# Attention scores: the product with the keys' low part moved to 64-row halves of the matmul array

## The chip, the cores and the metric

The kernel runs on one core of one Trainium2 chip. The metric is the device time of one execution in microseconds; three runs of the kernel before give a median of 1186.78 us. TensorE (PE in the profile) multiplies, VectorE (DVE), ScalarE (ACT) and GpSimd (POOL) work element by element, and SyncE (SP) issues most of the DMA transfers. A matmul record is preceded by a record of its weight load (PEld).

## The reference, cut to what matters

One transformer block on 1024 tokens of width 1024: a normalized and modulated input goes through one projection into a recurrent branch and an attention branch, both are mixed back, and a mixture of 16 experts follows. The part that the change touches is the attention:

```python
q = rms_norm(q, g_q) * (HEAD_DK ** -0.5)
k = rms_norm(k, g_k)
...
s = jnp.einsum('bqhjd,bkhjd->bhjqk', qi, k).astype(jnp.float32) + bias[None, :, None]
p = jax.nn.softmax(s, axis=-1)
w = (p[:, :, 0] - lam * p[:, :, 1]).astype(v.dtype)
return jnp.einsum('bhqk,bkhd->bqhd', w, v)
```

There are 4 heads (h), each with two score maps (j = 0, 1) over 64 channels (d), and queries are taken in 8 blocks of 128. All data is float32.

## The kernel before, in words

Products in float32 are made from parts: a value is split into a high part of type float32r and a low part, the rest. Each of the two goes through TensorE in one pass, and the products of parts are summed in PSUM.

For the attention, `proj_qk` writes the normalized and transposed queries and keys of each head to DRAM as `qkd[kind, h][part, channel, token]`; kind 0 is the queries, kind 1 the keys; part 0 is the high part, part 1 the low one; channels 0 to 63 belong to j = 0 and 64 to 127 to j = 1. `prep_begin(h)` (L725) loads them back into SBUF by 64-row transfers from SyncE's queue (L732): `qs[j]` has the high part of the queries on rows 0 to 63 and their low part on rows 64 to 127; `kh[j]` has the keys' high part on both row halves, `kl[j]` their low part on both. Four transfers of 256 KB each make a pair of tiles. With `qs` stationary, a matmul against `kh` over 128 rows is high times high plus low times high, and one against `kl` is high times low plus low times low.

`sc_mm(g, j)` (L755) makes the scores of one query block and one j: g counts the 32 turns (head times query block). It issues four matmuls of 512 columns into a [128, 1024] PSUM tile: `kh` for both column halves, then `kl` for both. `sc_max` (L764) adds the bias and takes the minimum (the queries carry a minus sign) in one VectorE instruction of 1024 columns; `sc_exp` is the exponential on ScalarE.

The loop over g (L908) has its orders of TensorE, VectorE and ScalarE written out by hand; a planner orders SyncE and GpSimd. In turn g TensorE makes: 8 transposes of turn g-2's weights (`w_tr`, tile `pw`), `sc_mm(g+1, 0)`, 16 matmul records of turn g-3's product with the values (`pv_mm`, tile `pv`), `sc_mm(g+1, 1)`, and in every fourth turn 4 transposes of a finished output (`o_out`, tile `po`). VectorE makes two `sc_max`, a few instructions of one column, and one combination of the two maps over 1024 columns (L807); every fourth turn it also begins a reciprocal root (`o_rstd`, L845 on) that waits for squares made on GpSimd (L837). GpSimd also prepares the output projection's weights in that loop (`load_wo(k)`, L875: a transfer, 4 products with `gate1`, and after ScalarE's rounding 4 subtractions into `wol`). `gate1` (L904) lies in memory that comes free when the last matmul of the V projection (tile `pjv`) has ended.

Turn 0's scores (`sc_first`, L776) stand inside that last V projection: TensorE waits there for the loads of `prep_begin(0)`, whose order is `kh`, `kl`, bias, `qs`. For h = 1 to 3 `prep_begin` runs 8 turns ahead, in the order `qs`, `kh`, `kl`, bias.

Elsewhere `mod_out` (L626) issues matmuls whose stationary operand has 32 columns, at four different column positions of the array (tile `mq`); all matmuls of the attention use the whole array, and no matmul of this kernel uses fewer than 128 rows.

Of the kernel before, what the change touches and what calls it, by code (L numbers as in the profile page):

```python
# [8 lines left out]
F32 = mybir.dt.float32  # L9
# [9 lines left out]
P = 128  # L19
# [63 lines left out]
def tile_block(ctx: ExitStack, tc, x, cols, w_mod, b_mod, w_in, wa, wx, lam_qk, relT, w_out, g2, w_router,  # L83
               w1, w3, w2, jbits, jfrac, out):
    nc = tc.nc
    V, A, G_, T, SY = nc.vector, nc.scalar, nc.gpsimd, nc.tensor, nc.sync
# [5 lines left out]
    def mm(out, lhsT, rhs, start, stop):  # L92
        return T.matmul(out, lhsT=lhsT, rhs=rhs, start=start, stop=stop)  # L93
# [26 lines left out]
    qkd = {(kind, h): dram.tile([2, P, S], F32, name=f"qkd{kind}{h}") for kind in range(2) for h in range(NH)}  # L120
# [350 lines left out]
    with tc.issue_after(i_act.ins), tc.issue_after(i_pool.ins):  # L471
        A.dma_start(out=jb, in_=jbits)
        A.dma_start(out=jf, in_=jfrac)
        for gi, src in enumerate((wa, wx)):
            braw = lt_(f"bd{gi}", [P, 8, P])
            G_.memset(braw, 0.0)
            for par in range(2):
                A.dma_start(out=braw[par * 64:par * 64 + 64, :, par * 64:par * 64 + 64],
                            in_=src.rearrange("(n par) c d -> par c n d", par=2)[par])
# [223 lines left out]
    prs = {}  # L703
# [6 lines left out]
    def qk_one(tag, name, dt=F32, shape=None):  # L710
        return qkp.tile(shape or [P, S], dt, tag=f"qk{tag}", bufs=1, name=name)

    def qk_tile(name, dt=F32):
        tg = qk_slot[name]
        if tg == "c":
            t_ = qk_one(tg, name, dt, [P, 2, S])
            return t_[:, 0, :], t_[:, 1, :]
        return [qk_one(f"{tg}{j}", f"{name}_{j}", dt) for j in range(2)]
# [6 lines left out]
    def prep_begin(h):  # L725
        sets = {}

        def load(tg, kind, parts):
            t_ = sets[tg] = qk_tile(f"{tg}{h}", F32R) if h else qk0[f"{tg}0"]
            for j in range(2):  # L730
                for a in range(2):
                    SY.dma_start(out=t_[j].bitcast(F32)[64 * a:64 * a + 64, :], in_=qkd[kind, h][parts[a], 64 * j:64 * j + 64, :])  # L732

        def bias():
            bt = sets["b"] = ap.tile([P, 1920], F32, name=f"bias{h}", tag="bias", bufs=1) if h % 2 else \
                qk_one("c", f"bias{h}", F32, [P, 1920]) if h else qk0["bias0"]
            src = bvd[h, 0:1920]
            SY.dma_start(out=bt, in_=bass.AP(tensor=src.tensor, offset=src.offset, ap=[[1, P], [1, 1920]]))

        qs, kh, kl = ("qs", 0, (0, 1)), ("kh", 1, (0, 0)), ("kl", 1, (1, 1))  # L740
        if h:
            for q in (qs, kh, kl):
                load(*q)
            bias()
        else:
            load(*kh)
            load(*kl)
            bias()
            load(*qs)
        prs[h] = (sets["b"], [sets[tg] for tg in ("qs", "kh", "kl")])  # L750
# [3 lines left out]

    def sc_mm(g, j):  # L755
        h, qt = divmod(g, NT)
        qs, kh, kl = (t_[j] for t_ in prs[h][1])
        sc_ = psa.tile([P, S], F32, tag="sc", bufs=2, name=f"sc{g}_{j}") if g else psb.tile([P, S], F32, tag="pg", bufs=2, name=f"sc0_{j}")
        for i, kk in enumerate((kh, kl)):
            for n in range(2):  # L760
                mm(sc_[:, n * 512:(n + 1) * 512], qs[:, qt * P:(qt + 1) * P], kk[:, n * 512:(n + 1) * 512], i == 0, i == 1)
        scp[g, j] = sc_

    def sc_max(g, j):  # L764
# [11 lines left out]
    def sc_first():  # L776
        for j in range(2):
            sc_mm(0, j)
        for j in range(2):
            sc_max(0, j)  # L780
            sc_exp(0, j)

    prep_begin(0)
    with tc.manual_schedule(engines={mybir.EngineType.PE}):
        proj_v(wv1, 1, vt[2:4], sc_first, AA)
# [121 lines left out]
    with tc.manual_schedule(engines={mybir.EngineType.PE, mybir.EngineType.DVE, mybir.EngineType.Activation}):  # L907
        for g in range(NG + 2):  # L908
            hn, u = divmod(g, 8)
            if u == 0 and hn + 1 < NH:  # L910
                prep_begin(hn + 1)
# [7 lines left out]
            n, st = divmod(g - 8, 4)  # L919
            if st == 0 and 0 <= n < 6:  # L920
                o_rstd(n)
            if g < NG:
                if g:
                    sc_exp(g, 0)
                if g + 1 < NG:
                    sc_mm(g + 1, 0)
                if g:
                    sc_max(g, 1)
# [10 lines left out]
            if g < NG - 1:  # L939
                sc_mm(g + 1, 1)  # L940
            if g in (4, 8, 12, 16, 24, 26, 28, 30):
                load_wo({4: 0, 8: 1, 12: 2, 16: 3, 24: 4, 26: 5, 28: 6, 30: 7}[g])
            n, st = divmod(g - 6, 4)
            if st == 0 and 0 <= n < 7:
                o_evac(n)
            n, st = divmod(g - 10, 4)
# [316 lines left out]
    raws, used, parts, raw_l = {}, [0], {}, []  # L1263
# [198 lines left out]
```

## Time and profile before

| | us |
|---|---|
| three runs: median (lowest to highest) | 1186.78 (1185.78 to 1189.39) |
| the profiled execution, and its span | 1189.59, 1187.8 |
| TensorE busy over the span | 1115.3 (94%) |
| VectorE busy | 955.2 (80%) |
| ScalarE busy | 791.6 (67%) |
| GpSimd busy | 484.1 (41%) |
| mean granted TensorE clock | 0.979 of full |

The page gives the share of each engine. The stretches matter more than the shares: the projections and the recurrent branch fill the time up to about 322 us, the attention loop that up to about 474 us, the mixing and the routing that up to about 618 us, and the experts the rest. The chain of waits is the work that ended last, followed back from the end: what stands in it at a time is what set the pace there.

### The profile page before, as it was taken

The page shows a single profiled execution, that of the slowest core. Times are in us where ns is not written, and L with a number is a line of the kernel's source. Part 1 is how long each engine was busy: PE and PEld are TensorE (multiplying, and loading weights), DVE is VectorE, ACT ScalarE, POOL GpSimd, SP SyncE. Part 2 cuts the span into 40 slices and gives each one's busy share as a digit, 9 for nine tenths or more (in the row PEclk, how much of TensorE's full clock was granted, in tenths as well). Part 3 has the DMA queues.
Part 4 walks back from the last instruction along what each step waited for, and adds up shares of the span by engine and source line. Part 5 has one row for each costly group of instructions (what it writes and reads, how often), then busy time and mean ns, then how long its engine had stood idle before and what let it go on. Part 6 is the DMA issues. An engine that isn't in the chain of part 4 may idle for free.

```text
span 1187.8 us, 17864 instructions
## 1 busy us (share of the span) xinstructions
PE 1115.3 (94%) x6319; PEld 935.9 (79%) x6320; DVE 955.2 (80%) x1241; ACT 791.6 (67%) x1046; POOL 484.1 (41%) x540
## 2 busy tenths in 40 slices
PE   6999899999699999999649999999999999999996
PEld 4699898888588899777538788888888888888885
DVE  6797657874298897444579999999999999999995
ACT  7548282394177788544318788878887888888784
POOL 4693232133087547243544334443324444322400
PEclk9899999999899999999969999999999999999999
DMA  9765725723844604534799999999999999999911
GB/s 334 225 195 171 238 72 186 241 71 63 203 108 117 176 6 143 186 113 163 263 337 345 358 377 385 392 408 393 375 394 393 367 397 406 394 394 387 392 46 18
DMA packets 147889, 303.82 MB, mean 256 GB/s; under 512 B 17996, under 2 KB 44748, under 8 KB 147796
## 3 DMA queue, kind: packets, MB, share of 16 engines
q1 hardware_dynamic: 134864, 279.46, 65.9%
q0 software_dynamic: 5488, 19.45, 6.4%
q10 hardware_dynamic: 7448, 3.77, 1.1%
q8 instruction: 50, 0.82, 0.3%
q14 instruction: 39, 0.32, 0.1%
HBM read 277.42 MB, written 25.22 MB: 255 GB/s over the span
## 4 chain that ended last, share of the span: by engine, by line
PE 73%; DVE 7%; DMA 6%; POOL 6%; issue 5%; ACT 2%; SPq 0%; POOLq 0%; ACTq 0%; DVEq 0%
PE ab L93 28%; PE y L93 13%; PE mix L93 7%; PE pjk L93 3%; PE pjz L93 3%; PE pv L93 3%; PE sc L93 3%; POOL wo L886 2%; PE pjv L93 2%; DMA wr<-in_w_mod_dram 2%; PE pw L814 1%; PE pjx L93 1%; PE pf L1346 1%; PE pg L93 1%; DVE macc L624 1%
## 5 line engine op out<-in xcount | busy, mean ns | idle before, releaser
L1246 POOL TENSOR_SCALAR oh<-iot,slot 128x128 bf16<-128x128 bf16 x120 | 146.3, 1234 | 252.2 <-PE pf L1346 252.2
L93 PE MATMUL ab<-wh,xeh 128*128 128x512 f32 x512 | 202.0, 395 | 0.2 <-ACT xeh L90 0.2
L93 PE MATMUL ab<-wh,xel 128*128 128x512 f32 x512 | 199.7, 390 | 0.1
L93 PE MATMUL ab<-wl,xeh 128*128 128x512 f32 x512 | 157.7, 389 | 0.0
L93 PEld LDWEIGHTS ab<-wl,xeh 128*128 128x128 f32 x512 | 96.1, 188 | 20.3
L93 PEld LDWEIGHTS ab<-wh,xel 128*128 128x128 f32 x512 | 96.2, 188 | 19.4 <-DVE xel L1259 0.5
L93 PEld LDWEIGHTS ab<-wh,xeh 128*128 128x128 f32 x512 | 96.1, 188 | 19.4 <-ACT xeh L90 0.5
L142 DVE TENSOR_TENSOR wl<-w_0r,wh 128x1024 fp32r<-128x1024 f32 x79 | 96.8, 1226 | 10.2 <-ACT wh L90 0.4
L90 ACT ACTIVATE wh<-w_0r 128x1024 fp32r<-128x1024 f32 x81 | 86.0, 1062 | 24.9 <-PE ab L93 14.9
L142 DVE TENSOR_TENSOR wl<-w_3r,wh 128x1024 fp32r<-128x1024 f32 x79 | 96.6, 1224 | 6.2
L90 ACT ACTIVATE wh<-w_1r 128x1024 fp32r<-128x1024 f32 x79 | 83.5, 1058 | 23.6 <-PE ab L93 18.9
L90 ACT ACTIVATE wh<-w_3r 128x1024 fp32r<-128x1024 f32 x79 | 83.9, 1062 | 21.9 <-PE ab L93 18.2
L142 DVE TENSOR_TENSOR wl<-w_2r,wh 128x1024 fp32r<-128x1024 f32 x80 | 96.3, 1220 | 2.4 <-ACT wh L90 0.5
L90 ACT ACTIVATE wh<-w_2r 128x1024 fp32r<-128x1024 f32 x80 | 84.7, 1060 | 18.9 <-PE ab L93 17.9
L142 DVE TENSOR_TENSOR wl<-w_1r,wh 128x1024 fp32r<-128x1024 f32 x78 | 92.6, 1220 | 3.8 <-ACT wh L90 2.1
L768 DVE CUSTOM_DVE_ANT_0 p<-sc,bias 128x1024 f32<-128x1024 f32 x64 | 77.7, 1214 | 18.0 <-PE sc L93 18.0
L93 PE MATMUL y<-wh,htl 128*128 128x512 f32 x256 | 82.9, 395 | 0.0
L93 PE MATMUL y<-wh,hth 128*128 128x512 f32 x256 | 80.9, 396 | 0.0
L93 PE MATMUL y<-wl,hth 128*128 128x512 f32 x256 | 79.6, 391 | 0.0
L90 ACT ACTIVATE p<-p,stat 128x1024 f32<-128x1024 f32 x62 | 70.8, 1151 | 4.8 <-DVE stat L768 4.8
L93 PEld LDWEIGHTS pv<-v,wt 128*128 128x128 f32 x512 | 61.7, 192 | 2.4
L93 PE MATMUL pv<-v,wt 128*128 128x128 f32 x512 | 62.1, 275 | 0.0
(458 smaller groups left out, 2858.5 us busy)
## 6 DMA issues: line engine op xcount, KB each, us to landing
w_0r<-in_w_dram SPq DMA_DIRECT2D x81, 512.0 KB, 8.5
w_1r<-in_w_dram SPq DMA_DIRECT2D x79, 512.0 KB, 8.8
w_2r<-in_w_dram SPq DMA_DIRECT2D x78, 512.0 KB, 9.0
w_3r<-in_w_dram SPq DMA_DIRECT2D x77, 512.0 KB, 8.7
wr<-in_w_mod_dram SPq DMA_DIRECT2D x32, 512.0 KB, 4.7
wi<-in_w_in_dram SPq DMA_DIRECT2D x18, 512.0 KB, 4.7
w_5r<-in_w_dram SPq DMA_DIRECT2D x17, 512.0 KB, 6.8
wm<-in_w_mod_dram SPq DMA_DIRECT2D x32, 256.0 KB, 4.9
```

The costliest lines, as they stand in the source:

```text
L90: return A.activation(out=out, in_=in_, func=func, **kw)
L93: return T.matmul(out, lhsT=lhsT, rhs=rhs, start=start, stop=stop)
L142: return (eng or V).tensor_tensor(out=lo, in0=src, in1=hi.bitcast(F32), op=ALU.subtract)
L624: V.scalar_tensor_tensor(out=macc[i], in0=w, scalar=sc[:, k:k + 1], in1=macc[i], op0=ALU.mult, op1=ALU.add)
L768: V.tensor_tensor_reduce(out=p_, in0=scp[g, j], in1=prs[h][0][:, b0:b0 + S], op0=ALU.add, op1=ALU.min, scale=1.0, scalar=3.0e38, accum_out ...
L814: T.transpose(pw[:, b * P:(b + 1) * P], pt_[g, 0][:, kt * P:(kt + 1) * P], ident)
L886: G_.tensor_tensor(out=r[:, qs], in0=r[:, qs], in1=gate1[:, qs], op=ALU.mult)
L1246: G_.tensor_scalar(out=oh[:, t, :], in0=iot, scalar1=slot[:, e, t:t + 1], scalar2=None, op0=ALU.is_equal)
L1346: T.transpose(pt[:, b * P:(b + 1) * P], sa[:, b * P:(b + 1) * P], ident)
```

## The change

`prep_begin` loads the tiles named `kl` in another form. Tile `kl[0]` now holds the keys' low part once: rows 0 to 63 have the first 512 tokens and rows 64 to 127 the last 512, with j = 0 in columns 0 to 511 and j = 1 in columns 512 to 1023. Tile `kl[1]`, called `dup` in `sc_mm`, holds the queries' high part a second time, with the j that `qs` has not on those rows. For j = 1, `qs` has its two parts in the other order (`a ^ j`). So for each j there is a copy of the queries' high part on rows 0 to 63 and one on rows 64 to 127.

In `sc_mm` the two matmuls against `kh` stay as they were. The two against `kl` now run over 64 rows: column half n = 0 on rows 0 to 63, n = 1 on rows 64 to 127. The product of the two low parts is no longer made. The four 256 KB transfers of `kl` become six: two of 256 KB (for `dup`) and four of 128 KB. Bytes, tiles and the count of matmuls stay the same.

```diff
-        def load(tg, kind, parts):
+        def load(tg, kind):
             t_ = sets[tg] = qk_tile(f"{tg}{h}", F32R) if h else qk0[f"{tg}0"]
             for j in range(2):
                 for a in range(2):
-                    SY.dma_start(out=t_[j].bitcast(F32)[64 * a:64 * a + 64, :], in_=qkd[kind, h][parts[a], 64 * j:64 * j + 64, :])
+                    rows = slice(64 * a, 64 * a + 64)
+                    if tg == "kl":
+                        if j == 0:
+                            SY.dma_start(out=t_[1].bitcast(F32)[rows, :], in_=qkd[0, h][0, 64 - 64 * a:128 - 64 * a, :])
+                        SY.dma_start(out=t_[0].bitcast(F32)[rows, j * 512:(j + 1) * 512],
+                                     in_=qkd[kind, h][1, 64 * j:64 * j + 64, a * 512:(a + 1) * 512])
+                    else:
+                        part = 0 if kind else a ^ j
+                        SY.dma_start(out=t_[j].bitcast(F32)[rows, :], in_=qkd[kind, h][part, 64 * j:64 * j + 64, :])
...
-        qs, kh, kl = (t_[j] for t_ in prs[h][1])
+        qs, kh = (t_[j] for t_ in prs[h][1][:2])
+        kl, dup = prs[h][1][2]
...
-        for i, kk in enumerate((kh, kl)):
-            for n in range(2):
-                mm(sc_[:, n * 512:(n + 1) * 512], qs[:, qt * P:(qt + 1) * P], kk[:, n * 512:(n + 1) * 512], i == 0, i == 1)
+        for n in range(2):
+            mm(sc_[:, n * 512:(n + 1) * 512], qs[:, qt * P:(qt + 1) * P], kh[:, n * 512:(n + 1) * 512], True, False)
+        for n in range(2):
+            rows = slice(64 * n, 64 * n + 64)
+            mm(sc_[:, n * 512:(n + 1) * 512], (qs if n == j else dup)[rows, qt * P:(qt + 1) * P], kl[rows, j * 512:(j + 1) * 512],
+               False, True)
```

## Rows read from the trace of the kernel before

**Rows 1.** Busy time by stretch: us, each engine's busy us (instructions), PEclk, DMA share, GB/s.

```profile
320.00:362.00 42.00, 38.65 (x251) 32.68 (x251) 35.66 (x63) 28.38 (x50) 31.55 (x45) 1.00 0.51 135
362.00:400.00 38.00, 37.57 (x264) 33.72 (x264) 33.96 (x66) 30.52 (x55) 26.35 (x48) 1.00 0.53 135
400.00:467.00 67.00, 66.76 (x475) 60.61 (x476) 61.55 (x120) 55.77 (x98) 35.97 (x75) 1.00 0.21 64
640.00:1140.00 500.00, 498.98 (x2400) 408.26 (x2399) 478.79 (x487) 402.55 (x431) 196.12 (x141) 1.00 1.02 380
```

**Rows 2.** Chain of waits, one turn of the attention loop: start us, us, what.

```profile
419.14 0.88 PE pw L814 x8
420.02 0.93 PE sc L93 x4
420.94 1.78 PE pv L93 x16
422.73 0.92 PE sc L93 x4
423.65 0.87 PE pw L814 x8
```

**Rows 3.** Waits of TensorE, 309 to 470 us: total us, times, longest.

```profile
PE sc L93 <- DMA qs<-qkd: 9.6, 2, 9.4
PE pw L814 <- DVE p L807: 2.6, 4, 1.0
PE sc L93 <- DVE stat L768: 1.4, 3, 0.7
```

**Rows 4.** Chain of waits, where GpSimd leads it.

```profile
327.55 17.17 POOL wo L886 x19
...
348.51 4.13 DMA wo<-in_w_out_dram
...
357.75 0.69 DVE hov L845
...
396.08 0.69 DVE hov L845
```

**Rows 5.** Timeline of TensorE, 355.9 to 400.5 us, first transposes of four turns: start us, us.

```profile
356.11 1.03 PE L814 MATMUL pw<-ident,p 128*128 128x128 f32 x8
...
361.90 1.06 PE L814 MATMUL pw<-ident,p 128*128 128x128 f32 x8 [0.40 <-DVE p L807]
...
394.61 1.04 PE L814 MATMUL pw<-ident,p 128*128 128x128 f32 x8
...
400.23 0.52 PE L814 MATMUL pw<-ident,p 128*128 128x128 f32 x3 [0.40 <-DVE p L807]
```

**Rows 6.** Timeline of TensorE around the 32-column group mq: start us, us.

```profile
266.52 0.71 PE L93 MATMUL pjz<-hh,wi_0h 128*128 128x512 f32 x2
267.16 1.07 PE L93 MATMUL mq<-macc,ones 128*32 128x512 f32 x8
268.16 0.74 PE L93 MATMUL pjz<-hl,wi_0h 128*128 128x512 f32 x2
268.73 0.62 PE L93 MATMUL pjz<-hh,wi_0l 128*128 128x512 f32 x2
```

**Rows 7.** Chain of the whole span: matmuls of 16 columns, a weight load each.

```profile
264.93 1.74 PE ps2w L93 x16
```

**Rows 8.** VectorE by line, 400 to 467 us: count, busy us, mean ns, idle before.

```profile
L768 DVE CUSTOM_DVE_ANT_0 p<-sc,bias 128x1024 f32<-128x1024 f32 x30 | 36.5, 1215 | 2.5 <-PE sc L93 2.5
```

**Rows 9.** Chain of waits ahead of the first scores.

```profile
286.68 14.19 DMA a2d<-a2c
...
303.79 7.78 DMA qs<-qkd
```

**Rows 10.** Timeline of SyncE, 299 to 303 us.

```profile
300.89 0.45 SPq L732 DMA_DIRECT2D kl<-qkd  x1
```

**Rows 11.** Busy time by stretch, as the first scores' data land.

```profile
309.00:312.00 3.00, 2.34 (x5) 1.49 (x6) 0.49 (x1) 0.00 (x0) 0.00 (x0) 0.50 1.06 232
```

More of the change, by code (lines that the diff above doesn't have):

```diff
@@ L738, in bias @@
             SY.dma_start(out=bt, in_=bass.AP(tensor=src.tensor, offset=src.offset, ap=[[1, P], [1, 1920]]))
-        qs, kh, kl = ("qs", 0, (0, 1)), ("kh", 1, (0, 0)), ("kl", 1, (1, 1))
+        qs, kh, kl = ("qs", 0), ("kh", 1), ("kl", 1)
         if h:
```

## The prediction, made before the change was run

> **What bounds the kernel now.** I began with the page's shares in the table above: TensorE is busy 94% of the span, VectorE 80%. A share is a mean over stages, so I next read the busy time by stretch around the code that changes. In the attention loop's second half, 400 to 467 us, TensorE is busy 66.76 us of 67 and VectorE 61.55 [rows 1]: TensorE has the pace, but VectorE has only 5.4 us of room, 8%. From 320 to 362 us TensorE leaves 3.4 us free, from 362 to 400 us 0.4 us [rows 1]. In the experts' stage it is busy 499 us of 500 [rows 1], so a shift of that stage's start should reach the end whole.
>
> Then the chain of waits. One plain turn of the loop, from one group of 8 transposes `pw` to the next, is 4.51 us, all on TensorE: `pw` 0.88, the four score matmuls of j = 0 0.93, the product with the values 1.78, the scores of j = 1 0.92 [rows 2]. A score matmul of 512 columns thus takes 0.232 us of TensorE's time. TensorE's waits in the loop are few: four for the combination of the maps (2.6 us) and three for a score buffer (1.4 us); the 9.6 us for `qs` are before the loop [rows 3]. The chain shows where most of the former come from: GpSimd's work on the output weights runs without a gap from the landing of `gate1` to 344.7 us, a transfer for it lands at 352.6, GpSimd then makes the squares for which VectorE waits until 357.75; the same happens once more until 396.08 [rows 4]. The turns behind these waits are long: 356.11 to 361.90 is 5.79 us, 1.3 more than a plain turn, and 394.61 to 400.23 is 5.62, 1.1 more [rows 5]. The stretches ahead of them are paced by GpSimd, not by TensorE.
>
> **The change part by part.** *The score matmuls.* Removed: two matmuls of 128 rows, 2 x 0.232 = 0.464 us, in each of 64 score maps (32 turns, 2 each). Added: two of 64 rows and 512 columns on different row halves. If they run at the same time they take about one pass, 0.22 to 0.24 us. No matmul of this kernel uses part of the rows, so what it costs to go from the whole array to half of it and back is not in the trace. The nearest row is the group `mq`: four matmuls with a 32-column stationary at four column positions, among ordinary ones [rows 6]. It shows both sides. The sharing works: four matmuls of 512 float32 columns leave eight records, and at the rate of the transposes (0.87 / 8 = 0.109 us for 128 float32 columns [rows 2], so 0.435 for 512) one after the other they would take 8 x 0.435 = 3.5 us, while `mq` starts at 267.16 and its successor at 268.16, 1.00 us: two rounds of four. But the switch costs: 1.00 is 0.13 more than two rounds of 0.435; the pair after it needs 0.57 (268.16 to 268.73) where a pair usually needs 0.46, 0.11 more; and the pair before it is 0.64 (266.52 to 267.16), 0.18 more, of which I put some 0.08 to that pair's own late start behind small matmuls. Together 0.34 to 0.42 us for one way in and back; I take 0.34.
>
> If row halves cost the same, the low part takes 0.34 + 0.22 = 0.56 us instead of 0.464: 0.10 us more for each map, not less. The bounds: without any switch cost the pair takes 0.24 us less (one pass of 0.232 saved); with the switch and the two halves one after the other it takes 0.34 + 0.435 - 0.464 = 0.31 us more. Between them lies a switch after which the two 128-column weight loads follow each other: 16 small matmuls with a weight load each take 1.74 us [rows 7], 0.11 us a load, which gives 0.21 us more. I take 0.10, by rows 6.
>
> The skill has a rule that speaks against the change: the Trainium skill, "TensorEngine Tiling (Array Packing)", section Key Properties, says that a change of the tiling mode, not merely of the tile, drains the engine. Rows 6 agree with that for column groups; no row here shows it for row groups.
>
> *What 0.10 us makes in the loop.* The 62 maps of turns 1 to 31 stand in it: 6.2 us. TensorE paces nearly all of it, but not the two GpSimd stretches. TensorE's time up to 357.75 us would grow by about 14 x 0.10 = 1.4 us, against the 1.3 us by which the turn there is too long; some 0.9 us more falls ahead of the second long turn, against its 1.1 us [rows 5]. GpSimd's chains don't get longer, so these two turns shrink, by up to 1.3 + 0.9 = 2.2 us: I take 1.9 us off, as not all of the growth falls ahead of the waits. Left: 4.3 us. VectorE and ScalarE only get more room.
>
> *The transfers of `kl`.* Six instead of four, the same bytes. For h = 1 to 3 they are issued 8 turns (36 us) ahead, and cost nothing: their cover is those turns. For h = 0 they are on the path: the chain goes through the transfer of `a2d` (14.19 us to 300.87), then the remaining issues of `prep_begin(0)`, then `qs` with 7.78 us to 311.57 [rows 9]. The last of the four `kl` transfers is issued at 300.89, right behind that wait [rows 10]; behind it on SyncE's queue stand the bias and the four `qs`. With six, if the fourth is again the one that waits, three are issued behind it instead of one. Bounds: 128 KB more at the 232 GB/s of that stretch [rows 11], 0.56 us, and two more issues of some 0.5 us, 1.1 us. I take 0.8 us; below nothing only if the wait falls on another transfer. This delays turn 0, the V projection's end, `gate1`, and with it GpSimd's first chain, so it isn't absorbed. In turn 0 itself TensorE is at 0.50 of its clock [rows 11]; a map more or less by 0.1 us there is nothing.
>
> *The dropped product* costs or saves nothing by itself: a matmul's time goes by its columns here, and low times low came in the same pass.
>
> **Sum.** +6.2 - 1.9 + 0.8 = +5.1 us. The profiled execution took 1189.59 us, which would become 1194.7. It is at the upper end of the three runs; against their median of 1186.78 the forecast is **1191.9 us**, slower by 0.4%. The case's own range: 0.06 to 0.13 us a map and 0.5 to 1.1 us at the start, +2.5 to +7.5 us.
>
> **The rivals.**
>
> *The halves run together and no switch is paid: faster.* Place: the same two matmuls. Price: 0.24 us saved a map, a turn of 4.04 us instead of 4.51. What decides is the switch: the change gains if way in and back cost under 0.24 us together, and loses above. For it: the two matmuls differ from their neighbours only in rows, and the column positions do run together in rows 6. The Trainium skill, "TensorE: Matmul & The Clock Gate", Part 3, says that weight loads for other row groups are pulled ahead and that matmuls on different row tiles start about 4 ns apart; by it the pair would cost one pass and nothing else. No row here shows it. Against it: rows 6. The gain would not be 62 x 0.24 = 15 us: VectorE has 61.55 us of work in the 67 us from 400 to 467 [rows 1], and its score instruction, 1.215 us, has waited only 2.5 us for scores there [rows 8]; I take two thirds of its 5.4 us of room, 3.6 us, and 0.9 us in the turns from 362 to 376 us; in the stretches that GpSimd paces, nothing. -4.5 + 0.8 = -3.7 us: **1183.1**, within -2 and -5.
>
> *The change doesn't do what it says: the halves follow each other.* With the switch paid, 0.31 us a map: 19.2 - 1.9 + 0.8 = +18 us, **1205**. With only the weight loads in series, 0.21 us: 13.0 - 1.9 + 0.8 = +11.9 us, **1198.7**. For it: nothing in the trace shows two row halves at once. Against it: the column positions in rows 6 go together, weight loads too.
>
> *Nothing changes in the loop:* the halves run in series without a switch, or a cheap switch eats what sharing saves. Then only the start counts: +0.8 us, **1187.6**.
>
> **How the numbers follow.** Forecast (switch as in rows 6, halves together) 0.48; no switch 0.25; parts in series 0.16 (loads 0.10, halves 0.06); nothing changes 0.11. A measurement of this kernel can tell about 0.3%, 3.6 us, from no change. The forecast lies above that in about 0.72 of its range: 0.35 slower, 0.13 same. The series cases are slower: 0.16. The gain of the first rival is capped right at the bound: 0.13 faster, 0.12 same. Nothing changes: 0.11 same. Sum: faster 0.13, same 0.36, slower 0.51. The range goes from 1182.8 (the first rival up to -4) to 1199.5 (loads in series), and leaves out the halves in series and the best of the gain. As both signs hold much of the chance, the likeliest case by itself is 1189.3 to 1194.3.
>
> **What the profile after would show.** Right: between the second `kh` matmul and the matmul after the low part about 0.55 to 0.6 us more than between ordinary ones; the two low matmuls start within some 10 ns of each other, their weight loads don't begin before the `kh` matmuls' time is over, and the next group starts late; plain turns of 4.7 us; fewer waits of VectorE for `osq`. Wrong in favour of the first rival: weight loads of the 64-row tiles beside the `kh` matmuls, turns near 4.3 us, VectorE over 95% busy, more waits of TensorE for `p` and score buffers. Wrong the other way: low matmuls 0.2 us or more apart. The start is right if `qs` lands 0.5 to 1.1 us later than 311.57, counted from the end of the `a2d` transfer. The sum would also fail if turns that are longer for TensorE move GpSimd's weight preparation behind a point where the mixing stage needs it.

## The result, and the profile after

The changed kernel is slower: 1195.17 us (median of 5 runs, 1193.51 to 1195.50) against 1186.89 us for the kernel before in the same comparison, a ratio of 1.0061 with a 95% interval of 1.0039 to 1.0083. That is 8.3 us between the medians, and 4.6 to 9.9 us by the interval. A second comparison of the same two (`after_again`, below) gave 1.0062, 1.0050 to 1.0075. The profiled execution has a span of 1193.2 us. One of the five runs of `e4_low_twice`, below, took 5066.76 us; it is left out of the median and the ratio given there.

The busy time by stretch shows TensorE without a gap from 362 us on, and VectorE, ScalarE and GpSimd busy for a smaller share of the last stretch than before (VectorE 60.77 of 70 us against 61.55 of 67); the columns are those of [rows 1]:

```profile
320.00:362.00 42.00, 39.73 (x250) 28.07 (x250) 36.57 (x65) 28.89 (x50) 32.09 (x48) 1.00 0.50 136
362.00:400.00 38.00, 38.00 (x261) 28.90 (x259) 33.95 (x67) 29.71 (x52) 25.82 (x45) 1.00 0.51 134
400.00:470.00 70.00, 70.00 (x471) 52.41 (x471) 60.77 (x117) 55.52 (x98) 35.08 (x73) 1.00 0.18 58
```

The chain of waits gives one turn of the attention loop, as [rows 2] did before:

```profile
415.93 1.02 PE pw L826 x8
416.95 0.89 PE sc L93 x4
417.84 1.98 PE pv L93 x16
419.82 0.90 PE sc L93 x4
420.72 1.02 PE pw L826 x8
```

From `pw` to `pw` it is 4.79 us instead of 4.51. The four score matmuls look no longer than before (0.89 and 0.90 against 0.93 and 0.92), but the groups that follow them do: `pw` went from 0.88 to 1.02, `pv` from 1.78 to 1.98. The timeline of TensorE and of its weight loads shows why, around one map:

```profile
414.79 0.71 PE L93 MATMUL sc<-kh,qs 128*128 128x512 f32 x2
415.43 0.50 PE L93 MATMUL sc<-kl,kl 64*128 64x512 f32 x1
415.43 0.50 PE L93 MATMUL sc<-kl,qs 64*128 64x512 f32 x1
415.86 0.66 PE L826 MATMUL pw<-ident,p 128*128 128x128 f32 x4
```

```profile
414.76 0.30 PEld L93 LDWEIGHTS sc<-kh,qs 128*128 128x128 f32 x2
415.42 0.18 PEld L93 LDWEIGHTS sc<-kl,kl 64*128 64x128 f32 x1 [0.36 <-issue]
415.43 0.18 PEld L93 LDWEIGHTS sc<-kl,qs 64*128 64x128 f32 x1
415.86 0.53 PEld L826 LDWEIGHTS pw<-ident,p 128*128 128x128 f32 x5 [0.25 <-issue]
```

The two 64-row matmuls start together, at 415.43, and so do their weight loads. But these loads start only after an idle 0.36 us of the load path, when the `kh` matmuls' time is nearly over, and the next group's first weights again only after 0.25 us. In the kernel before, where all four are full matmuls, the weights for `kl` are loaded 0.23 us ahead of their matmuls, beside the running `kh` ones (its timeline, weight loads and TensorE):

```profile
415.59 0.42 PEld L93 LDWEIGHTS sc<-kl,qs 128*128 128x128 f32 x2
415.82 0.62 PE L93 MATMUL sc<-kl,qs 128*128 128x512 f32 x2
```

At each change of rows that cover is lost: the loads start within 0.01 us of their matmuls.

The two long turns of [rows 5] are gone:

```profile
357.00 1.09 PE L826 MATMUL pw<-ident,p 128*128 128x128 f32 x8
361.79 1.09 PE L826 MATMUL pw<-ident,p 128*128 128x128 f32 x8
...
391.49 1.04 PE L826 MATMUL pw<-ident,p 128*128 128x128 f32 x8
396.24 1.09 PE L826 MATMUL pw<-ident,p 128*128 128x128 f32 x8
401.03 1.09 PE L826 MATMUL pw<-ident,p 128*128 128x128 f32 x8
```

The same two turns are 357.00 to 361.79 and 396.24 to 401.03 here, plain turns of 4.8 us. The waits of VectorE for GpSimd's squares say the same, first before, then after, from the first transposes to the last (total us, times, longest):

```profile
DVE hov L845 <- POOL osq L837: 4.2, 3, 1.9
```

```profile
DVE hov L857 <- POOL osq L849: 1.0, 2, 0.5
```

One measure will be used for all kernels below: *the loop*, from the start of the first `pw` group to that of the last. Here are its ends, before and after:

```profile
328.83 1.06 PE L814 MATMUL pw<-ident,p 128*128 128x128 f32 x8 [0.76 <-DVE p L807]
473.02 1.04 PE L814 MATMUL pw<-ident,p 128*128 128x128 f32 x8
```

```profile
328.36 1.06 PE L826 MATMUL pw<-ident,p 128*128 128x128 f32 x8 [0.59 <-DVE p L819]
477.08 1.04 PE L826 MATMUL pw<-ident,p 128*128 128x128 f32 x8
```

So 144.2 us before and 148.7 after, +4.5 us. The loop is a far sharper measure than the whole time: ahead of it the same work ends up to 6 us earlier or later from one profiled execution to the next (the `a2d` store begins between 283.7 and 289.9 us in the kernels shown here), and the granted clock in the two places where it is at half stays there for a varying time (about 10 and 27 us in the profile of before, 14 and 31 in that of the changed kernel).

### The profile page after: what moved, and what is told of

Read it like the earlier page. It is cut to its first block, busy times and chain, and to the rows that moved or that the text cites. A ratio compares the mean times of both kernels' runs of the same rounds, so it can differ in the third digit from the quotient of the medians.

```text
span 1193.2 us, 17878 instructions
## 1 busy us (share of the span) xinstructions
PE 1123.0 (94%) x6320; PEld 920.0 (77%) x6320; DVE 953.8 (80%) x1241; ACT 792.0 (66%) x1046; POOL 485.0 (41%) x540
## 4 chain that ended last, share of the span: by engine, by line
PE 78%; DVE 9%; DMA 6%; issue 4%; ACT 2%; POOL 1%; SPq 0%; POOLq 0%; DVEq 0%; ACTq 0%
PE ab L93 28%; PE y L93 13%; PE mix L93 7%; PE pv L93 5%; PE sc L93 4%; PE pjk L93 3%; PE pw L826 3%; DMA wr<-in_w_mod_dram 2%; PE pjz L93 2%; DVE macc L624 2%; PE pjv L93 2%; PE pjx L93 2%; PE pf L1358 1%; PE pg L93 1%; DMA a2d<-a2c 1%
## 5 line engine op out<-in xcount | busy, mean ns | idle before, releaser
L142 DVE TENSOR_TENSOR wl<-w_0r,wh 128x1024 fp32r<-128x1024 f32 x79 | 96.8, 1226 | 10.2 <-ACT wh L90 0.4
L90 ACT ACTIVATE wh<-w_3r 128x1024 fp32r<-128x1024 f32 x79 | 83.9, 1062 | 21.9 <-PE ab L93 17.6
L90 ACT ACTIVATE wh<-w_2r 128x1024 fp32r<-128x1024 f32 x80 | 84.7, 1060 | 19.1 <-PE ab L93 17.6
L780 DVE CUSTOM_DVE_ANT_0 p<-sc,bias 128x1024 f32<-128x1024 f32 x64 | 77.9, 1218 | 23.3 <-PE sc L93 23.2
L93 PE MATMUL pv<-v,wt 128*128 128x128 f32 x512 | 65.1, 281 | 0.0
```

The source lines that it names most:

```text
L90: return A.activation(out=out, in_=in_, func=func, **kw)
L142: return (eng or V).tensor_tensor(out=lo, in0=src, in1=hi.bitcast(F32), op=ALU.subtract)
L780: V.tensor_tensor_reduce(out=p_, in0=scp[g, j], in1=prs[h][0][:, b0:b0 + S], op0=ALU.add, op1=ALU.min, scale=1.0, scalar=3.0e38, accum_out ...
```

## The experiments

All kernels, in the order in which they are told; times as a ratio to the kernel before in the same comparison, with the 95% interval, and the loop from each profile:

| kernel | median us | ratio (interval) | loop us |
|---|---|---|---|
| before | 1186.89 | | 144.2 |
| changed | 1195.17 | 1.0061 (1.0039 to 1.0083) | 148.7 |
| `e1_loads_only` | 1188.58 | 1.0008 (0.9992 to 1.0023) | 144.2 |
| `e2_rows_only` | 1194.74 | 1.0071 (1.0045 to 1.0097) | 148.7 |
| `e3_one_half` | 1206.19 | 1.0156 (1.0122 to 1.0191) | 161.8 |
| `e4_low_twice` | 1207.93 | 1.0191 (1.0148 to 1.0234) | 161.9 |
| `after_again` | 1195.12 | 1.0062 (1.0050 to 1.0075) | 148.7 |
| `e5_one_switch` | 1192.01 | 1.0039 (1.0024 to 1.0054) | 144.6 |
| `e6_before_a2d` | 1188.31 | 1.0013 (1.0001 to 1.0024) | 144.1 |
| `e7_after_a2d` | 1192.55 | 1.0043 (1.0030 to 1.0056) | 148.7 |
| `before_again` | 1187.79 | 1.0013 (0.9996 to 1.0029) | 143.5 |
| `e9_before_rstd` | 1186.64 | 0.9998 (0.9982 to 1.0015) | 141.8 |
| `e10_one_switch_rstd` | 1186.04 | 0.9992 (0.9978 to 1.0007) | 140.3 |
| `e10_again` | 1184.35 | 0.9972 (0.9957 to 0.9988) | 140.3 |

### Which part loses: the loads alone, the rows alone

`e1_loads_only` has the loads of the changed kernel and full matmuls:

```diff
-            rows = slice(64 * n, 64 * n + 64)
-            mm(..., (qs if n == j else dup)[rows, qt * P:(qt + 1) * P], kl[rows, j * 512:(j + 1) * 512], False, True)
+            mm(..., qs[:, qt * P:(qt + 1) * P], (kl, dup)[j][:, n * 512:(n + 1) * 512], False, True)
```

> The loads of the changed kernel with 128-row matmuls as before; the two matmuls against the kl tiles multiply wrong data, so the scores are not the reference's. Theory (the six kl transfers of head 0 delay qs on SyncE's queue): turns of the attention loop stay at 4.50 us, qs lands about 12.2 us after the end of the a2d transfer instead of 10.7, and the time is 1.5 to 3 us above before. Rival (the later start in the profile after was chance of that execution): qs 10.7 us after a2d, time within 1 us of before.

The loop is that of before, and the time +1 us, -1 to +2.7: it excludes neither the theory (1.5 to 3 us) nor the rival (within 1 us).

What the loads do to the first scores has to be read from the same transfer in each trace, counted from the end of the `a2d` store, and the chains name two different ones. In the kernel before the chain goes through the `qs` transfer for turn 0's second map (10.70 us after the store's end, [rows 9]); here it goes through the one for the first map (9.26 us), so that the 12.2 us of the expectation and this 9.26 can't be compared. The start of the first score matmul can. In the kernel before it is 8.55 us after the store's end at 300.87; in the changed kernel, whose store ends at 297.62, 10.15 us (TensorE before; the changed kernel's chain; its TensorE):

```profile
309.42 1.19 PE L93 MATMUL sc<-kh,qs 128*128 128x512 f32 x2 [9.36 <-DMA qs<-qkd]
```

```profile
284.43 13.19 DMA a2d<-a2c
```

```profile
307.77 1.19 PE L93 MATMUL sc<-kh,qs 128*128 128x512 f32 x2 [9.96 <-DMA qs<-qkd]
```

In the profiles that leave the store where it was, this takes 8.4 to 8.6 us in the five kernels with four `kl` transfers and 9.2 to 10.2 us in the seven with six (9.4 in this one), 1.1 us more on the average. The chains through the second map's transfer say the same: 10.7 to 10.8 us with four, 11.3 to 12.2 with six. So the theory holds for the start, with about 1.1 us.

`e2_rows_only` is the other half: the loads of before, and 64-row matmuls:

```diff
-        for i, kk in enumerate((kh, kl)):
-            for n in range(2):
-                mm(..., qs[:, qt * P:(qt + 1) * P], kk[:, n * 512:(n + 1) * 512], i == 0, i == 1)
+        for n in range(2):
+            mm(..., qs[:, qt * P:(qt + 1) * P], kh[:, n * 512:(n + 1) * 512], True, False)
+        for n in range(2):
+            rows = slice(64 * n, 64 * n + 64)
+            mm(..., qs[rows, qt * P:(qt + 1) * P], kl[rows, n * 512:(n + 1) * 512], False, True)
```

> The matmuls of the changed kernel on the loads of before: 64 rows, the column halves on different row halves; for the second column half it is low times low instead of high times low. Theory (each way into 64 rows and back costs TensorE 0.42 us while the halves run together): turns of 4.79 us as in the changed kernel, the two long turns at 356 and 395 us gone, qs 10.7 us after a2d; time 4.5 to 6.5 us above before. Rival (the loads carry most of the loss): turns near 4.5 us and less than 2 us above before.

Its chain has the turn of the changed kernel to the hundredth:

```profile
414.12 1.02 PE pw L816 x8
415.14 0.89 PE sc L93 x4
416.03 1.98 PE pv L93 x16
418.01 0.90 PE sc L93 x4
418.91 1.02 PE pw L816 x8
```

The loop is 148.7 us and the time 1.0071, 8.4 us more (5.3 to 11.5); 4.5 to 6.5 was expected. The loop's loss belongs to the rows, not to the loads.

### What in the rows: switch or halves

`e3_one_half` puts both column halves on rows 0 to 63, so that they can't share the array; its loads are those of before:

```diff
+            mm(..., qs[0:64, qt * P:(qt + 1) * P], kl[0:64, n * 512:(n + 1) * 512], False, True)
```

> The loads of before; both column halves of the low product on rows 0 to 63, so that they can't run together. Theory (halves together in the changed kernel): the second half adds a pass of 0.21 to 0.23 us a map: turns of 5.2 us, time 4.79 to 5.2 over 31 turns = 13 us above the rows-only kernel, about 18 us above before. Rival (the halves were never together): turns of 4.79 us and the time of the rows-only kernel, 5 us above before.

`e4_low_twice` issues the pair of the changed kernel twice in a row, `for i in range(2)` around it.

> The changed kernel with the pair of 64-row matmuls issued twice in a row, so that the low product is counted twice in the scores. Theory (the cost is the switch, paid once however many pairs follow): one more round of 0.22 us a map, turns of 5.2 us, 62 x 0.22 = 13 to 14 us above the changed kernel, 21 us above before. Rival (the cost is in each 64-row pair, whose matmuls or weight loads are slow by themselves): 0.4 to 0.6 us more a map, turns of 5.6 to 6.0 us, 25 us or more above the changed kernel.

TensorE in `e3_one_half`, from one `pw` to the next `pv`, then in `e4_low_twice` over the same stretch of a turn:

```profile
427.78 0.71 PE L93 MATMUL sc<-kh,qs 128*128 128x512 f32 x2
428.42 0.73 PE L93 MATMUL sc<-kl,qs 64*128 64x512 f32 x2
429.08 2.05 PE L93 MATMUL pv<-v,wt 128*128 128x128 f32 x16
```

```profile
426.17 0.71 PE L93 MATMUL sc<-kh,qs 128*128 128x512 f32 x2
426.81 0.50 PE L93 MATMUL sc<-kl,qs 64*128 64x512 f32 x1
426.81 0.50 PE L93 MATMUL sc<-kl,kl 64*128 64x512 f32 x1
427.15 0.39 PE L93 MATMUL sc<-kl,qs 64*128 64x512 f32 x1
427.15 0.39 PE L93 MATMUL sc<-kl,kl 64*128 64x512 f32 x1
427.47 2.05 PE L93 MATMUL pv<-v,wt 128*128 128x128 f32 x16
```

Two matmuls on one row half take 0.66 us from their start to `pv` (428.42 to 429.08), and four on two halves take the same 0.66 (426.81 to 427.47). Both kernels have plain turns of 5.26 to 5.27 us, 0.47 to 0.48 above the 4.79 of the changed kernel: 0.24 us a map for one more round, whether the round holds one matmul or two. So the halves do run together, fully, and a second pair pays no second switch. This prices the switch: the low part costs 0.464 + 0.145 = 0.61 us a map (0.464 before, and half of 4.79 - 4.50), less a round of 0.24: **0.37 us** for one way into 64 rows and back. Both theories held, and both rivals fall. The loops are 17.6 us and 17.7 us longer than that of before, and the times 18.5 us (14.5 to 22.7) and 22.7 us (17.6 to 27.8); the second interval only just reaches its loop.

### How much of the loss is the loop

`after_again` is the changed kernel once more.

> The changed kernel once more, to size its loss. Theory (the loss is the loop, 148.7 us from the first to the last transposes against 144.2, and little else): 4.5 to 6 us above before. Rival (something outside the loop costs as well, in the start or behind the loop): 7 us or more.

5.9 to 8.9 us above before by its interval, with the same loop of 148.7 us: the loop explains 4.5 of it, or 5.2 against the second profile of before (143.5), and that lies under the interval, on the rival's side. To see how level such comparisons are, the kernel before ran under another name:

> The kernel before under another name, to see what the comparison gives where nothing is changed. Theory (comparisons are level, and the rest of the loss behind the loop's 4.5 us is real): within 1 us of before. Rival (a kernel set beside before looks slower by itself): 1.5 us or more above it.

It came out 1.5 us above before, with an interval of -0.5 to +3.4, so neither side of that expectation is excluded. With the loop at 4.5 us and about 1.1 us at the start, some 2 to 3 us of the loss have no place in these traces.

### Fewer switches

If a switch costs 0.37 us, one a turn instead of two should bring TensorE's turn to about 4.42 us, below the 4.50 of before. `e5_one_switch` makes both maps of a turn together, where the second stood:

```diff
-                if g + 1 < NG:
-                    sc_mm(g + 1, 0)
...
-                sc_mm(g + 1, 1)
+                sc_mm(g + 1, 0, 1)      # kh for both j, then the 64-row pairs of both
```

> The changed kernel with the score matmuls of both maps of a turn together: kh of both, then the 64-row pairs of both, so that there is one way into 64 rows and back in a turn instead of two. Theory (a switch costs 0.375 us, whatever is between): TensorE's work in a plain turn falls from 4.79 to 4.42 us, below the 4.50 of before; the loop takes 141 to 145 us and the time is within -3 and +1 us of before. Rival (VectorE gets the scores of j = 0 later, and waits for them): turns of 4.6 us or more, with waits of VectorE for sc in most turns, and slower than before by 2 us or more.

Most turns are 4.34 to 4.47 us as expected (4.9 where the output's transposes stand in them), but every turn with the reciprocal root is 5.2 to 5.9 us, so that the loop is 144.6 us: 4.1 less than the changed kernel, level with before. The wait is on the other side now. TensorE wants a score buffer that VectorE hasn't read, because the root stands between VectorE's two score instructions (TensorE's timeline):

```profile
374.58 0.71 PE L93 MATMUL sc<-kh,qs 128*128 128x512 f32 x2
375.58 0.73 PE L93 MATMUL sc<-kh,qs 128*128 128x512 f32 x2 [0.29 <-DVE stat L783]
```

Between 309 and 480 us these waits make 5.0 us, in the changed kernel 0.6. The wait that the rival named, VectorE for scores, hardly grew (9.2 us against 8.8 from 326 us on). So the price of the switch and the loop are the theory's, but the time is the rival's: 2.8 to 6.4 us above before, where the theory had -3 to +1. The loop doesn't show that loss; the profile is of the fastest of the six runs (1187.50 us, the others up to 1193.57), so where the slower ones lose it stays open.

`e9_before_rstd` and `e10_one_switch_rstd` move the root (`o_rstd`) behind the combination of the maps on VectorE, and `o_out` one turn later, in the kernel before and in `e5_one_switch`:

```diff
-            n, st = divmod(g - 8, 4)
-            if st == 0 and 0 <= n < 6:
-                o_rstd(n)
...
             if 1 <= g <= NG:
                 comb2(g - 1)
+            n, st = divmod(g - 8, 4)
+            if st == 0 and 0 <= n < 6:
+                o_rstd(n)
...
-            n, st = divmod(g - 10, 4)
+            n, st = divmod(g - 11, 4)
```

> The kernel before with the reciprocal root (o_rstd) behind the combination of the maps on VectorE instead of between its two score instructions, and the transposes of the finished output one turn later. Theory (the long turns of before, 5.79 and 5.62 us, come from VectorE waiting for GpSimd's squares ahead of a score instruction, and this is what the changed kernel absorbed): both fall to 5.0 us or less, the loop takes 140.5 to 142.5 us instead of 144.2, and the time is 1.5 to 3.5 us below before. Rival (GpSimd's work itself paces these stretches, and the wait only moves): the loop stays at 143.5 us or more.

> The kernel with one switch a turn, with o_rstd moved in the same way. Theory (with one switch TensorE has 4.37 us of work in a plain turn, and the turns of 5.24 us were VectorE's, which had the root between its two score instructions): turns with the root fall to 4.9 us or less, the loop takes 138.5 to 141.5 us, 1 to 3 us less than the kernel before with the move. Rival (VectorE's work, 4.3 us a turn on average, is the bound wherever the root stands): loop of 143 us or more, no gain over the kernel before with the move.

In `e9_before_rstd` the first long turn is gone and the second is shorter but still there, one turn later as the root is:

```profile
358.33 1.03 PE L814 MATMUL pw<-ident,p 128*128 128x128 f32 x8
362.97 1.04 PE L814 MATMUL pw<-ident,p 128*128 128x128 f32 x8
...
395.40 1.03 PE L814 MATMUL pw<-ident,p 128*128 128x128 f32 x8
400.65 0.60 PE L814 MATMUL pw<-ident,p 128*128 128x128 f32 x4
```

358.33 to 362.97 is 4.64 us, 395.40 to 400.65 is 5.25. The loop is 141.8 us, 1.7 to 2.4 less than in the two profiles of before: VectorE's wait for the squares was part of what the long turns cost, not all. The time doesn't tell it from before (-2.1 to +1.8 us; 1.5 to 3.5 below was expected). In `e10_one_switch_rstd` the six long turns fall to 4.4 to 4.8 us, and the loop is 140.3 us, 1.5 less than with the move alone and 8.4 less than in the changed kernel. Its time was not clear of before at first, so it ran once more:

> The kernel with one switch a turn and the root moved, once more. Theory (its loop is 3 to 4 us shorter than that of before, and nothing else differs): loop of 140 to 141 us and 1 to 4 us below before. Rival (the shorter loop is given back elsewhere): within 1 us of before or above it.

The loop is 140.3 us again, and the time 0.9972 (0.9957 to 0.9988), 1.4 to 5.1 us below before. Taken with the first comparison (-2.6 to +0.8 us) this version is clearly faster than the changed kernel. Against the kernel before it is some 1 to 3 us faster, clear of noise in one comparison of two.

### The start

`e6_before_a2d` and `e7_after_a2d` issue the `a2d` store from GpSimd's queue:

```diff
-        A.dma_start(out=a2d[:, :].rearrange("o (k p) -> p (o k)", p=P), in_=a2c)
+        G_.dma_start(out=a2d[:, :].rearrange("o (k p) -> p (o k)", p=P), in_=a2c)
```

> The kernel before with one thing moved: the 4 KB store of a2d is issued from GpSimd's queue instead of ScalarE's. Theory (the fourth kl transfer of head 0 waits for that store alone, and qs stands behind it): no gap in the issues of prep_begin(0), TensorE's wait of 9.4 us for qs falls under 3 us, the granted clock doesn't fall to half there, 8 to 13 us faster than before. Rival (the transfers or memory that comes free late set the landing of qs): qs lands at most 3 us sooner after the a2d store begins, less than 3 us faster.

> The changed kernel with the same move of the a2d store. Theory (the loop's loss is independent of the start): the loop takes 148.7 us as in the changed kernel, and the kernel is 4.5 to 5.5 us slower than the kernel before with the move, where the delay of the two extra issues falls away. Rival (part of the loss sits in the start): less than 4 us slower than it.

SyncE's queue in `e6_before_a2d` has no wait behind `kl` any more, and the first `qs` transfer goes out at 289.92 instead of 302.02 us; yet the chain goes through `qs` to 305.80 (SyncE's timeline, then the chain):

```profile
285.97 2.51 SPq L732 DMA_DIRECT2D kl<-qkd  x4
288.94 0.33 SPq L738 DMA_DIRECT2D bias<-bvd  x1
289.92 15.33 SPq L732 DMA_DIRECT2D qs<-qkd  x8
```

```profile
289.92 15.88 DMA qs<-qkd
305.80 1.14 issue
306.94 2.05 PE sc L93 x4
```

TensorE waits 9.1 us there, before 9.4. From the begin of the `a2d` store to the first score matmul it is 22.2 us; in the two profiles of before it is 22.7 and 21.3. The theory fell: the store's end is what SyncE waited for, but the transfers issued 12 us earlier landed no sooner, and the kernel isn't faster.

`e7_after_a2d` has the loop of 148.7 us. It is 4.2 us above `e6_before_a2d` by the medians and 3.6 us by the ratios; its theory (4.5 to 5.5) and the rival (under 4) aren't told apart by that. Its first score matmul begins 19.8 us after the store, in the two profiles of the changed kernel 23.3 and 22.8, so in this one execution the move did take 3 us off. This points to the start as the place of the rest of the loss; `e1_loads_only` (+1 us) and `e2_rows_only` (5.3 to 11.5 us above before without any change to the loads) point away from it. It stays open.

## Why the prediction was right or wrong

It was right in its sign, and the measured 1195.17 us lies within its range (1182.8 to 1199.5) but just above the likeliest case's own (1189.3 to 1194.3): +8.3 us between the medians against a forecast of +5.1. Point by point:

*What bounds the loop.* Right. TensorE had the pace, and the 0.145 us more in each of two maps came out in the turn (4.79 us against 4.50); VectorE and ScalarE only got room.

*The switch.* The mechanism was right, and read from the right row: the 32-column group `mq` [rows 6] showed both that parts of the array run together and that it costs to get in and out. The Trainium skill's rule of a drain at each change of mode ("TensorEngine Tiling (Array Packing)", Key Properties), which spoke against the change, agrees with what these runs show for row halves: a switch costs 0.37 us in `e3_one_half` and `e4_low_twice`, and the load path stands idle for 0.36 and 0.25 us at the two changes in the profile after. The size was off: I took 0.34 and a pass of 0.22, and got 0.10 us a map; it was 0.37 and 0.24, and 0.145. I had set 0.08 us of the way in aside as the first pair's own late start, and so took the lower end of my 0.34 to 0.42, and I priced the pass below the 0.232 us that [rows 2] give for it. Over the 62 maps this is 2.8 us too little. The six maps at the loop's two ends, 0.9 us, should not have been counted: the first turn and the last two take the same time in both kernels.

*What GpSimd's stretches take back.* The mechanism was right: VectorE's waits for the squares fell from 4.2 to 1.0 us. The size was off here too. In the other 28 turns 28 x 0.29 = 8.1 us of growth came out as 4.6, so 3.5 us were absorbed where I took 1.9: next to the turns of 5.79 and 5.62 us also five lesser ones that took 0.2 to 0.3 us more than a plain turn. My 0.9 us for the second long turn was also too small by my own rate: from 361.90 to 394.61 us [rows 5] stand 7 turns, 14 maps, 1.4 us, enough for all of its 1.1. So the loop's +4.5 us stands beside a forecast of 6.2 - 1.9 = 4.3 by luck, as the sum of errors: 2.8 us too little for the maps, 0.9 us too much for the ends and 1.6 us too little cover.

*The start.* Right in its mechanism, a little small: forecast 0.8 us, within 0.56 to 1.1; measured 1.1 us between the means of kernels with four and with six transfers. As forecast, the fourth of the six waits, so that three are issued behind the wait instead of one; in the changed kernel the two more issues take 0.64 us each, where I had some 0.5. The landing at 311.57 that I took for the first scores' data is that of turn 0's second map; the first scores begin at 309.42. By that later landing the sign I had set is missed: the changed kernel's is 1.5 us later, not 0.5 to 1.1. The time of `e1_loads_only` (-1 to +2.7 us) can't show any of it.

*The rivals.* "No switch is paid" is excluded by the weight loads and by the turns. "Halves or loads in series" are excluded by matmuls and weight loads that start together, and by `e3_one_half`, which shows what series would have cost: turns of 5.26 us. "Nothing changes in the loop" is excluded by its 148.7 us.

*What is left.* Loop and start make some 5.6 us, inside the first interval (4.6 to 9.9) and just under the second (5.9 to 8.9). A kernel against its own copy gave +1.5 us (-0.5 to +3.4). Behind the loop's last transposes the spans have 716.1 and 716.0 us left in the two profiles of the changed kernel and 714.8 and 714.9 in the two of before, but 714.8 and 715.1 in `e2_rows_only` and `e7_after_a2d`, which have the same loop as the changed kernel; so the rest isn't shown to lie there. `e5_one_switch` has such a rest too. Whether it is a real cost outside the loop the runs don't settle.

## What to carry to other kernels

Half the rows of the array are half free only if the array stays in that shape: price a matmul on part of the rows with the way in and back (0.37 us here, more than one pass of 512 columns at 0.24), and put as many as can be between one way in and the way back. The second pair of matmuls in a row cost a plain round and no switch, and gathering two maps' pairs behind one switch, with VectorE's other work moved out of the way of its score reads, turned a loop of 148.7 us into one of 140.3. Part of that is the moved work: alone, it took the loop of before from 144.2 to 141.8. A slower engine also fills waits that were there before: count those, or the cost of an edit comes out too large.

## What the runs showed of the hardware

- A change between 128-row and 64-row matmuls costs about the same as one between full and 32-column ones: 0.37 us for both ways, against 0.34 to 0.42 in [rows 6]. At each change the next weights aren't loaded beside the running matmul: the load path is idle for 0.36 us on the way in and 0.25 us on the way back.
- Two 64-row matmuls of 512 columns on different row halves start within 10 ns and cost one round of 0.24 us; their weight loads start together too (415.42 and 415.43).
- Unexpected: with SyncE's wait ahead of `qs` gone, the first score matmul came no sooner: 22.2 us after the `a2d` store began, against 22.7 and 21.3. What holds the transfers up then isn't shown.
